# A hybrid decoder block: the first tap and the edge columns of its short convolution move from VectorE to ScalarE

## The chip, the core and the metric

The kernel runs on one core of a Trainium2 chip. The metric is the device time of one execution in microseconds (us), given as the median of several runs. A core has one matrix engine (TensorE; PE in the profile, its weight loads PEld), three engines for element work (VectorE or DVE, ScalarE or ACT, GpSimd or POOL) and a queue that issues the transfers (SyncE or SP). Each engine works through its own instructions in the order in which they stand in its queue and waits, where needed, for semaphores of the others.

## What is computed

One decoder layer on 2048 positions of width 1024, in float32. Both head groups, the output projection, a SwiGLU feed-forward part and three RMS norms are in it. The part that matters here is head group B, a gated causal convolution of width 3 over positions:

```python
h = rmsnorm(x, norm1_g[l])
proj = h @ w_in[l]
p_q, p_k, p_v, p_g, p_a, c_b, c_c, c_h = jnp.split(proj, splits, axis=-1)
...
o = gla_chunked(q, k, v, log_a)          # head group A
...
u = c_c * c_h
o_conv = c_b * causal_depthwise_conv(u, conv_w[l])
mixed = jnp.concatenate([o_gla, o_conv], axis=-1) @ w_out[l]
x = x + mixed
...
def causal_depthwise_conv(u, w):
    """u: (B,S,C), w: (CONV_K, C). y_t = sum_j w_j * u_{t-(CONV_K-1)+j}."""
    u_pad = jnp.pad(u, ((0, 0), (CONV_K - 1, 0), (0, 0)))
    y = w[0] * u_pad[:, 0:seq]
    for j in range(1, CONV_K):
        y = y + w[j] * u_pad[:, j:j + seq]
```

So position t needs u at t-2, t-1 and t: a block of positions needs the last two columns of the block to its left.

## The kernel before

Channels lie on the 128 partitions and positions on the free axis. The 2048 positions are four blocks of 512 (`PB`), handled as two halves of two blocks. In `in_proj(half, ops, first)` twelve *units* run one after the other. A unit multiplies 256 output channels with both blocks of the half by a scheme of seven 512-wide block products instead of eight (`PRODUCTS`, `unit`, lines 344 to 382). Each product is a run of 12 matmuls of 128x512: float32 is split into a high and a low part (`split`, line 144), and for each k the order is high·high (line 340), high·low (line 341), low·high (line 342). The weights of a unit are split when they have arrived: ScalarE copies the high part (line 145), VectorE subtracts it for the low part (line 146), and GpSimd builds the sums that the scheme needs (lines 323, 324, 325 and 330). Products that are read out go from PSUM to SBUF on ScalarE (line 360) or are added on VectorE (line 364). A PSUM bank can be written again only after it has been read, so TensorE waits for these.

The last six units are the convolution: for `i0` = 0 and 2 the units of c_c, c_h and c_b. After the unit of c_h a loop runs over two channel tiles (`r`) and the two blocks of the half (`j`). It multiplies u = c_c * c_h into a tile of 514 columns (line 577), copies the two columns on the left from `halo` (line 578), copies the tile's own last two columns back into `halo` (line 579), forms the first tap into y (line 581), which takes the place of c_c, and adds the second and third tap (line 583). That makes four passes of four tiles; in time they lie at 210 to 238, 271 to 296, 491 to 521 and 573 to 594 us. After the unit of c_b the result is multiplied with it (line 588), split and stored (lines 590 to 593) for the output projection.

Beside the units run pieces of background work that `tick()` advances after each product: `h1_ahead` (norm and split of the second half's input, with `scaled` on line 464, GpSimd differences on lines 246 to 259 and `split`), the forget gate (`forget_gate`, lines 531 to 550) and the chunks of the linear attention (`gla_half`: scores on line 640, transposes on lines 646, 649 and 700, outputs on lines 664 and 666, state on lines 681 and 682, carry on line 656, norm on lines 688 to 693). The program is not issued in source order: a scheduler with its own timeline orders each engine's queue when the program is built, so an edit at one place can move instructions of the units and of the background work around it. The feed-forward part (`ffn_up`, `ffn_down`) follows from about 855 us on.

Waits of TensorE that the prediction names belong to these names: `wq` is a split weight quarter (`weight_quarter`), `c` a product that was read out, `raw` the weights as they come from memory, `osb` a normalised chunk of the attention that is transposed on line 700.

Of the kernel before, what the change touches and what calls it, by code (L numbers as in the profile page):

```python
# [13 lines left out]
AF = mybir.ActivationFunctionType  # L14
ALU = mybir.AluOpType
# [6 lines left out]
PB = 512  # L22
# [20 lines left out]
C_G1, C_G2, C_GF, C_BG, C_GN, C_CW = 0, 8, 16, 24, 26, 27  # L43
# [4 lines left out]
def tile_hymba_block(ctx, tc, x, xt, win, wa, wgu, wout, wffn, wdown, wdown_first, small, out):  # L48
    nc = tc.nc
    act, dve, pool, pe = nc.scalar, nc.vector, nc.gpsimd, nc.tensor  # L50
# [42 lines left out]
    halo = mixer.tile([P, 4, 2], F32, name="halo")  # L93
# [30 lines left out]
    def col(c):  # L124
        return sml[:, c : c + 1]
# [13 lines left out]
    def store(dst, src):  # L139
        return nc.sync.dma_start(dst, src)  # L140
# [3 lines left out]
    def split(src, hi, lo):  # L144
        last_hi[:] = [act.activation(hi, src, AF.Copy)]  # L145
        return dve.tensor_tensor(lo, src, hi.bitcast(F32), ALU.subtract)  # L146
# [197 lines left out]
    def unit(src, ops, into=None):  # L344


        w = unit_weights(src)

        def mul(i, o=None):
            first = o is None  # L350
            o = bank() if first else o
            n, m = PRODUCTS[i]
            for k in range(len(ops[m])):
                product_step(o, w[n], ops[m], k, first)
            tick()
            return o

        def copied(name, o, at):
            t = tt(name) if into is None else into[at]
            act.activation(t[:], o[:], AF.Copy)  # L360
            return t

        def plus(t, o):
            dve.tensor_tensor(t[:], o[:], t[:], ALU.add)  # L364
            return t


        oa = mul(0)
        c11 = copied("c11", oa, (0, 0))
        ob = mul(1)  # L370
        c22 = copied("c22", ob, (1, 1))
        mul(2, oa)
        c12 = copied("c12", oa, (0, 1))
        plus(c11, mul(3))
        mul(4, oa)
        plus(c22, oa)
        mul(5, ob)
        plus(c12, ob)
        mul(6, oa)
        if into is not None:  # L380
            copied("c21", oa, (1, 0))
        return [(0, 0, c11, False), (1, 1, c22, False), (0, 1, c12, False), (1, 0, oa, True)]

    def settled(c, in_psum):

        if not in_psum:
            return c
        s = tt("c11")
        act.activation(s[:], c[:], AF.Copy)
        return s  # L390
# [3 lines left out]
    def silu(c, in_psum):  # L394
        s = tt("sg") if in_psum else c
        last_silu[:] = [act.activation(s[:], c[:], AF.Silu)]
        return s
# [156 lines left out]
    def in_proj(half, ops, first):  # L554
        def units():
            for u in range(12):
                with ExitStack() as stack:
                    if half == 0 and u == 1:
                        stack.enter_context(tc.issue_after(last_load[0].ins))
                    yield first if u == 0 and first else unit(win[u], ops)  # L560

        units = units()
        for dst, i0 in ((s_kq, 0), (s_kq, 2), (s_v, 0), (s_v, 2)):
            for r, j, c, p in next(units):
                store(dst[2 * half + j][i0 + r][:], settled(c, p)[:])
        for i0 in (0, 2):
            for r, j, c, p in next(units):
                store(s_g[2 * half + j][i0 + r][:], silu(c, p)[:])
        background.append(gla_half(half))
        for i0 in (0, 2):  # L570
            cc = {(r, j): settled(c, p) for r, j, c, p in next(units)}
            ch = {(r, j): c for r, j, c, _ in next(units)}
            for r in range(2):
                i = i0 + r
                for j in range(2):
                    s = tp.tile([P, PB + 2], F32, name="u", tag="t")
                    dve.tensor_tensor(s[:, 2:], ch[r, j][:], cc[r, j][:], ALU.mult)
                    dve.tensor_copy(s[:, 0:2], halo[:, i, :])
                    dve.tensor_copy(halo[:, i, :], s[:, PB : PB + 2])
                    y = cc[r, j]  # L580
                    dve.tensor_scalar(y[:], s[:, 0:PB], col(C_CW + i), None, ALU.mult)
                    for n in (1, 2):
                        dve.scalar_tensor_tensor(
                            y[:], s[:, n : n + PB], col(C_CW + 4 * n + i), y[:], ALU.mult, ALU.add
                        )
            for r, j, c, _ in next(units):
                y = cc[r, j]
                dve.tensor_tensor(y[:], c[:], y[:], ALU.mult)
                hi = tp.tile([P, PB], F32R, name="hi", tag="t")
                split(y[:], hi[:], y[:].bitcast(F32R))  # L590
                dst = s_mix[2 * half + j][i0 + r]
                store(dst[:, 0, :], hi[:].bitcast(F32))
                store(dst[:, 1, :], y[:])


    def gla_half(half):
        chunks = [(b, t) for b in (2 * half, 2 * half + 1) for t in range(PT)]
        with tc.issue_after(last_silu[0].ins):
            tables = act.preload_act_table_set("natural_log_exp_and_others")
        with tc.issue_after(tables.ins):  # L600
            nxt = gla_load(*chunks[0])
        o = None
        for n, (b, t) in enumerate(chunks):
            cur = nxt
            s = gla_scores(b, t, *cur)
            yield
            if o is not None:
                gla_finish(*chunks[n - 1], *o)
                yield
            if n + 1 < len(chunks):  # L610
                nxt = gla_load(*chunks[n + 1])
            o = gla_outputs(b, t, *s)
            yield
        gla_finish(b, t, *o)
        done.add((b, t))
        yield
# [315 lines left out]
    def last_unit(src, ops, b12, y, ssq):  # L932
# [62 lines left out]
        ]  # L995
    )
    in_proj(0, ops, first)
    drain_background(lambda: len(background) < 2)
    ops = load_pairs(s_h1)
    background.append(gate(1, ops))  # L1000
    in_proj(1, ops, None)
    drain_background(lambda: (1, PT - 1) in done)
    ssq = out_proj(0, build_mix(0))
# [118 lines left out]
```

## Time and profile before

| | us |
|---|---|
| median of 3 runs | 2133.78 (2132.6 to 2134.49) |
| the profiled execution | 2132.17 |
| span of the profiled execution | 2130.3 |
| mean granted TensorE clock in it | 0.986 of full speed |
| matmuls of the units, lines 340 to 342, busy | 984.6 + 977.6 + 969.8 |
| ScalarE product copies, line 360, busy | 156.3 (270 of them) |
| VectorE additions of products, line 364, busy | 185.0 (270 of them) |

The profile holds one execution. Rows of a timeline read: start, duration, engine, line, operation, output<-input, shapes and types, and in brackets the idle time of the engine just before it with what ended it. Rows of a table by stretches of time read: the stretch, its length, then the busy time of PE, PEld, DVE, ACT and POOL with the number of instructions, the granted clock, the share of the transfer engines and GB/s; a table restricted to one line shows only the engines that the line uses. A row of a line reads: duration in ns as minimum/median/maximum, and when the first and the last started.

### The profile page before, as it was taken

How to read it: one execution, taken by the hardware profiler on the slowest of the kernel's cores; microseconds unless marked ns; L12 is line 12 of the kernel's file. 1: busy time of each engine (PE TensorE's matmuls, PEld its weight loads, DVE VectorE, ACT ScalarE, POOL GpSimd, SP SyncE). 2: the span in 40 equal slices, each digit the busy share in tenths (PEclk: the TensorE clock that was granted, in tenths of full speed). 3: DMA queues.
4: the chain of work that ended last, by engine and by line, in shares of the span. 5: the costliest groups of instructions: out<-in, count | busy, mean ns of one | idle time of the engine just before them, and what ended most of it. 6: DMA issues, size and time to landing. Idle time of an engine off the chain costs nothing.

```text
span 2130.3 us, 26959 instructions
## 1 busy us (share of the span) xinstructions
PE 2048.0 (96%) x9137; PEld 1656.0 (78%) x9137; DVE 1435.2 (67%) x2035; ACT 1005.8 (47%) x1959; POOL 983.5 (46%) x707
## 2 busy tenths in 40 slices
PE   6899999999999999999999999999999999999996
PEld 4677787887788887778788887887888888887875
DVE  7768875558663586887887564554786777664554
ACT  6455344565543334654555453333454454553344
POOL 3526422221102364555555346874644555435774
PEclk9999999999999999999999999999999999999998
DMA  7349587433495981655554577698365445587662
GB/s 281 114 136 328 189 314 228 149 105 110 145 334 175 362 297 70 212 230 195 222 218 180 219 301 265 246 348 351 125 221 204 151 176 197 190 333 276 267 266 109
DMA packets 190987, 470.80 MB, mean 221 GB/s; under 512 B 19968, under 2 KB 65280, under 8 KB 181248
## 3 DMA queue, kind: packets, MB, share of 16 engines
q1 hardware_dynamic: 190848, 469.07, 60.9%
q8 instruction: 72, 1.18, 0.2%
q14 instruction: 67, 0.55, 0.1%
HBM read 300.70 MB, written 168.30 MB: 220 GB/s over the span
## 4 chain that ended last, share of the span: by engine, by line
PE 76%; DMA 9%; DVE 8%; ACT 3%; issue 2%; POOL 1%; SPq 1%; DVEq 0%; ACTq 0%; POOLq 0%
PE mm L340 22%; PE mm L342 22%; PE mm L341 22%; DVE wq L146 2%; PE mm L740 2%; PE mm L741 2%; PE mm L743 2%; DVE op L146 1%; DVE h L464 1%; DMA op<-sa_B 1%; DMA raw<-in_wdown_dram 1%; DMA op<-shT 1%; PE a_ps L515 1%; DVE so L146 1%; DMA sx<-y 1%
## 5 line engine op out<-in xcount | busy, mean ns | idle before, releaser
L340 PE MATMUL mm<-op,wq 128*128 128x512 f32 x2495 | 984.6, 396 | 27.7 <-ACT c L360 16.9
L342 PE MATMUL mm<-op,wq 128*128 128x512 f32 x2495 | 969.8, 394 | 16.1 <-DVE wq L146 15.4
L341 PE MATMUL mm<-op,wq 128*128 128x512 f32 x2495 | 977.6, 392 | 1.1 <-DVE op L146 1.1
L146 DVE TENSOR_TENSOR wq<-raw,wq 128x512 fp32r<-128x512 f32 (+2 forms) x628 | 533.6, 855 | 306.8 <-ACT wq L145 304.3
L145 ACT ACTIVATE wq<-raw 128x512 fp32r<-128x512 f32 (+2 forms) x628 | 366.7, 588 | 583.2 <-PE mm L342 422.8
L340 PEld LDWEIGHTS mm<-op,wq 128*128 128x128 f32 x2495 | 472.1, 189 | 147.9 <-ACT c L360 22.8
L342 PEld LDWEIGHTS mm<-op,wq 128*128 128x128 f32 x2495 | 472.1, 189 | 126.1 <-DVE wq L146 26.8
L341 PEld LDWEIGHTS mm<-op,wq 128*128 128x128 f32 x2495 | 472.7, 189 | 99.0 <-DVE op L146 1.9
L325 POOL TENSOR_TENSOR raw<-s,raw 128x512 f32<-128x512 f32 (+2 forms) x98 | 128.5, 1312 | 439.4 <-DVE wq L146 392.4
L364 DVE TENSOR_TENSOR c<-mm,c 128x512 f32<-128x512 f32 x270 | 185.0, 685 | 114.0 <-PE mm L342 111.4
L323 POOL TENSOR_TENSOR s<-raw 128x512 f32<-128x512 f32 (+2 forms) x98 | 131.1, 1338 | 190.6 <-DMA raw<-in_wffn_dram 91.4
L330 POOL TENSOR_TENSOR raw<-raw 128x512 f32<-128x512 f32 (+2 forms) x98 | 128.1, 1307 | 139.0 <-DVE wq L146 118.2
L360 ACT ACTIVATE c<-mm 128x512 f32<-128x512 f32 x270 | 156.3, 585 | 29.9 <-PE mm L342 29.2
L722 POOL TENSOR_TENSOR ssx<-ssx,q 128x512 f32<-128x512 f32 x52 | 75.1, 1457 | 152.5 <-ACT q L721 152.4
L324 POOL TENSOR_TENSOR raw<-raw 128x512 f32<-128x512 f32 (+2 forms) x98 | 138.3, 1411 | 4.5
L902 POOL TENSOR_TENSOR y<-c,y 128x512 f32<-128x512 f32 x66 | 99.2, 1505 | 68.5 <-DVE c L364 68.4
L146 DVE TENSOR_TENSOR so<-t,so 128x512 fp32r<-128x512 f32 x100 | 95.1, 959 | 20.5 <-ACT so L145 20.4
L145 ACT ACTIVATE wq<-s 128x512 fp32r<-128x512 f32 (+2 forms) x98 | 57.6, 587 | 97.1 <-PE mm L342 94.6
L740 PE MATMUL mm<-op,wq 128*128 128x512 f32 x256 | 100.7, 394 | 0.0
L741 PE MATMUL mm<-op,wq 128*128 128x512 f32 x256 | 99.8, 390 | 0.0
L146 DVE TENSOR_TENSOR wq<-s,wq 128x512 fp32r<-128x512 f32 (+2 forms) x98 | 83.8, 855 | 15.5 <-ACT wq L145 15.1
L145 ACT ACTIVATE so<-t 128x512 fp32r<-128x512 f32 x100 | 62.6, 628 | 44.8 <-DMA sa_B<-so 21.6
(173 smaller groups left out, 1884.3 us busy)
## 6 DMA issues: line engine op xcount, KB each, us to landing
raw<-in_wffn_dram SPq DMA_DIRECT2D x44, 1024.0 KB, 5.9
sa_T<-so SPq DMA_DIRECT2D x88, 512.0 KB, 4.6
op<-sa_T SPq DMA_DIRECT2D x88, 512.0 KB, 9.6
sa_B<-so SPq DMA_DIRECT2D x69, 512.0 KB, 3.4
op<-sa_B SPq DMA_DIRECT2D x69, 512.0 KB, 9.3
raw<-in_win_dram SPq DMA_DIRECT2D x23, 1024.0 KB, 5.4
raw<-in_wdown_dram SPq DMA_DIRECT2D x24, 768.0 KB, 5.8
sx<-y SPq DMA_DIRECT2D x48, 256.0 KB, 4.6
```

The lines of the kernel that those rows point to most:

```text
L145: last_hi[:] = [act.activation(hi, src, AF.Copy)]
L146: return dve.tensor_tensor(lo, src, hi.bitcast(F32), ALU.subtract)
L323: pool.tensor_tensor(s1, a21, a22, ALU.add)
L324: pool.tensor_tensor(a21, a11, a21, ALU.subtract)
L325: pool.tensor_tensor(a11, s1, a11, ALU.subtract)
L340: pe.matmul(o[:], wh, xh, start=first and k == 0, stop=False, skip_group_check=True)
L341: pe.matmul(o[:], wh, xl, start=False, stop=False, skip_group_check=True)
L342: return pe.matmul(o[:], wl, xh, start=False, stop=k == n - 1, skip_group_check=True)
L360: act.activation(t[:], o[:], AF.Copy)
L364: dve.tensor_tensor(t[:], o[:], t[:], ALU.add)
L740: pe.matmul(o[e, j][:], wh, m[:, 0, :], start=k == 0, stop=False)
L741: pe.matmul(o[e, j][:], wh, m[:, 1, :], start=False, stop=False)
```

## The change

The first tap becomes a ScalarE copy with a per-partition scale, and the copies of the two edge columns become ScalarE copies. The second block of a half (`j` = 1) takes its two left columns from the first block's tile `s` rather than from `halo`, and `halo` is written once for each channel tile, after both blocks, and in the first half only. The product, the second and third tap and everything else are as they were; lines below the edit shift by three.

```diff
@@ -572,17 +572,20 @@
             for r in range(2):
                 i = i0 + r
+                left = halo[:, i, :]
                 for j in range(2):
                     s = tp.tile([P, PB + 2], F32, name="u", tag="t")
                     dve.tensor_tensor(s[:, 2:], ch[r, j][:], cc[r, j][:], ALU.mult)
-                    dve.tensor_copy(s[:, 0:2], halo[:, i, :])
-                    dve.tensor_copy(halo[:, i, :], s[:, PB : PB + 2])
+                    act.activation(s[:, 0:2], left, AF.Copy)
+                    left = s[:, PB : PB + 2]
                     y = cc[r, j]
-                    dve.tensor_scalar(y[:], s[:, 0:PB], col(C_CW + i), None, ALU.mult)
+                    act.activation(y[:], s[:, 0:PB], AF.Copy, scale=col(C_CW + i))
                     for n in (1, 2):
                         dve.scalar_tensor_tensor(
                             y[:], s[:, n : n + PB], col(C_CW + 4 * n + i), y[:], ALU.mult, ALU.add
                         )
+                if half == 0:
+                    act.activation(halo[:, i, :], left, AF.Copy)
```

## The prediction

> **What bounds the kernel now.** I read the page's busy shares first, then its chain of waits, then a table of stretches around the four convolution passes, and last the timeline of each engine inside them.
>
> ```profile
> PE 2048.0 (96%) x9137; PEld 1656.0 (78%) x9137; DVE 1435.2 (67%) x2035; ACT 1005.8 (47%) x1959; POOL 983.5 (46%) x707
> PE 76%; DMA 9%; DVE 8%; ACT 3%; issue 2%; POOL 1%; SPq 1%; DVEq 0%; ACTq 0%; POOLq 0%
> 200.00:240.00 40.00, 35.69 (x141) 27.70 (x141) 38.99 (x59) 17.44 (x32) 19.35 (x12) 0.91 0.77 257
> 270.00:295.00 25.00, 25.00 (x119) 20.47 (x118) 20.95 (x40) 8.42 (x16) 5.90 (x4) 1.00 0.72 266
> 485.00:520.00 35.00, 34.16 (x143) 26.11 (x142) 29.53 (x59) 15.79 (x32) 5.76 (x4) 1.00 0.26 81
> 520.00:545.00 25.00, 22.63 (x130) 18.45 (x129) 21.43 (x40) 14.40 (x37) 5.72 (x4) 1.00 0.60 195
> 570.00:595.00 25.00, 25.00 (x134) 20.54 (x133) 23.48 (x55) 12.81 (x37) 3.75 (x2) 1.00 0.72 247
> ```
>
> TensorE is busy for 96% of the span and carries the chain, so VectorE time is worth something only where TensorE waits for it. The first number after a stretch is its length, the second TensorE's busy time. In the second and fourth pass (270 to 295, 570 to 595) TensorE is busy throughout: nothing can be gained there. The first pass (200 to 240, VectorE 39 of 40 us) leaves 4.3 us of gaps, and its granted clock is 0.91. The third leaves 0.8 us; behind it, at 520 to 545, lie 2.4 us. The timeline names these gaps; the bracket is the wait before the row and what ended it:
>
> ```profile
> 217.47 0.50 PE L342 MATMUL mm<-op,wq 128*128 128x512 f32 x1 [0.62 <-DVE wq L146]
> 226.03 0.50 PE L342 MATMUL mm<-op,wq 128*128 128x512 f32 x1 [2.82 <-DVE wq L146]
> 227.63 0.63 PE L342 MATMUL mm<-op,wq 128*128 128x512 f32 x1
> 230.18 0.80 PE L340 MATMUL mm<-op,wq 128*128 128x512 f32 x1 [0.64 <-ACT c L360]
> 233.76 0.62 PE L342 MATMUL mm<-op,wq 128*128 128x512 f32 x1
> 515.75 0.50 PE L342 MATMUL mm<-op,wq 128*128 128x512 f32 x1 [0.84 <-DVE wq L146]
> 539.62 0.50 PE L340 MATMUL mm<-op,wq 128*128 128x512 f32 x1 [2.37 <-ACT c L360]
> 873.76 0.50 PE L342 MATMUL mm<-op,wq 128*128 128x512 f32 x1 [3.01 <-DVE wq L146]
> 874.10 0.40 PE L340 MATMUL mm<-op,wq 128*128 128x512 f32 x1
> ```
>
> So 0.62 + 2.82 + 0.64 + 0.84 + 2.37 = 7.3 us of waits are within reach. One thing hangs on them. After the wait of 2.82 the matmuls from 227.63 to 233.76 last 0.63 instead of 0.40: the lower clock costs (1 - 0.91) x 35.69 = 3.2 us. After the wait of 3.01 at 873.76 the next one lasts 0.40, and the stretch that holds the wait of 2.37 has a clock of 1.00. A wait of this length therefore sometimes brings the slow clock and sometimes not; I treat it as a chance event of one execution.
>
> The Trainium skill, "TensorE: Matmul & The Clock Gate", section "HAM oscillation — how this bites in real kernels", puts the limit at gaps above about 3.4 us; its section "What's actually happening" says that the activity window is free-running. By the first, 2.82 would have cost no clock and shortening it would be worth its length alone; the trace disagrees there, and the rows decide. The second would explain why 3.01 went unpunished.
>
> **What the change removes and adds.** The rows of the removed lines, then the nearest rows for what ScalarE gets:
>
> ```profile
> L578 DVE COPY u<-halo x16: 151/158/1294, 211.1 to 587.9; 128x2 f32<-128x2 f32 x16
> L579 DVE COPY halo<-u x16: 151/158/1268, 212.4 to 589.8; 128x2 f32<-128x2 f32 x16
> L581 DVE TENSOR_SCALAR c<-u,sml x16: 470/476/1593, 213.2 to 589.8; 128x512 f32<-128x512 f32 x16
> L942 ACT ACTIVATE y<-y,sml 128x512 f32<-128x512 f32 x16 | 11.2, 715 | 0.2
> L150 ACT ACTIVATE hl<-hsq 128x4 f32<-128x4 f32 x16 | 3.3, 206 | 3.5 <-DVE hsq L689 3.2
> ```
>
> By medians VectorE loses 16 x (0.158 + 0.158 + 0.476) = 12.7 us. ScalarE gains 16 taps, 16 left copies and 4 halo writes (two channel tiles for each of the first half's two passes): 16 x 0.715 + 20 x 0.206 = 15.6 us, 3.9 us a pass. Line 942 is the same operation, size and per-partition scale as the tap; the bounds of a tap are 0.58 (product copies of this width, 156.3 us over 270) and 0.72. ScalarE is free for 22.6 of 40, 16.6 of 25, 19.2 of 35 and 12.2 of 25 us in the passes' rows, so 3.9 us fit into each; that idle time is the cover. If it were gone, all 15.6 us would lie on ScalarE's queue ahead of weight halves and product copies. No transfer is added or removed, and PE and transfers differ in order only near the passes; the feed-forward part issues as before.
>
> **First pass.** What ends the wait of 2.82 is the last low part of a weight quarter, VectorE's 225.29 row:
>
> ```profile
> 218.68 0.68 DVE L364 TENSOR_TENSOR c<-mm,c 128x512 f32<-128x512 f32 x1
> 219.28 1.64 DVE L146 TENSOR_TENSOR lo<-t,hi 128x512 fp32r<-128x512 f32 x1
> 220.84 1.78 DVE L146 TENSOR_TENSOR wq<-raw,wq 128x512 fp32r<-128x512 f32 x1
> 222.54 1.24 DVE L579 COPY halo<-u 128x2 f32<-128x2 f32 x1
> 223.69 0.47 DVE L581 TENSOR_SCALAR c<-u,sml 128x512 f32<-128x512 f32 x1
> 224.09 1.28 DVE L146 TENSOR_TENSOR lo<-h,hi 128x512 fp32r<-128x512 f32 x2
> 225.29 0.68 DVE L146 TENSOR_TENSOR wq<-raw,wq 128x512 fp32r<-128x512 f32 x1
> 219.08 1.29 POOL L323 TENSOR_TENSOR s<-raw 128x512 f32<-128x512 f32 x1 [3.09 <-DMA raw<-in_win_dram]
> 220.44 1.62 POOL L324 TENSOR_TENSOR raw<-raw 128x512 f32<-128x512 f32 x1
> 222.03 1.72 POOL L259 TENSOR_TENSOR t<-h,t 128x512 f32<-128x512 f32 x1
> ```
>
> Three VectorE operations here take about 1.1 us too long (1.64 and 1.78 against 0.68; the two-column copy 1.24 against 0.158), each while a GpSimd operation runs: the engines take turns. What VectorE can give back is therefore its own operations, not the turns of GpSimd, which stay three. In the changed program the queue behind the 218.68 addition holds five operations up to the awaited one: a low part, a quarter, a low part, a second tap, the quarter. Before it held seven: a low part, a quarter, copy, first tap, two low parts, the quarter. One low part moved ahead (0.62 by starts), copy (0.08 by its pitch) and tap (0.40) left, one second tap (0.68) came in: 0.62 + 0.08 + 0.40 - 0.68 = 0.4 us earlier. The tap waits on ScalarE for the product u; behind it in that queue stand the high parts of the next quarters, due about 2.5 us later by my walk, so they stay covered. Bounds: the whole wait goes (-2.8), or a GpSimd turn more, half a piece long, slips in (+0.5). I take -0.4, nearest the summed rows. The 0.62 before it gains at most itself, but it lies ahead of the same second wait, which then grows by as much: 0. The 0.64 for a product copy stays.
>
> **Third pass.** The awaited quarter is VectorE's 515.02 row:
>
> ```profile
> 510.91 1.27 DVE L579 COPY halo<-u 128x2 f32<-128x2 f32 x1
> 515.02 0.68 DVE L146 TENSOR_TENSOR wq<-raw,wq 128x512 fp32r<-128x512 f32 x1
> ```
>
> A copy of 1.27 leaves the queue ahead of it, but its turn with GpSimd passes to its neighbour; with one tap's 0.40 and 0.08 for the copy it is 0.5 us earlier: -0.5 (bounds -0.84, all of it; +0.3, a ScalarE tap late by 0.715 against VectorE's 0.47).
>
> **Behind the third pass.** The wait of 2.37 ends with a product copy that stands in ScalarE's queue behind the attention's carry, and that waits for VectorE's state:
>
> ```profile
> 529.05 2.98 DVE L146 TENSOR_TENSOR c<-c,hi 128x512 fp32r<-128x512 f32 x3
> 531.95 1.78 DVE L146 TENSOR_TENSOR wq<-raw,wq 128x512 fp32r<-128x512 f32 x1
> 534.18 1.47 DVE L146 TENSOR_TENSOR c<-c,hi 128x512 fp32r<-128x512 f32 x1
> 536.60 0.81 ACT L656 ACTIVATE carry<-state,em 64x128 f32<-64x128 f32 x2 [3.29 <-DVE state L682]
> 536.87 0.39 PE L342 MATMUL mm<-op,wq 128*128 128x512 f32 x1
> 538.99 0.58 ACT L360 ACTIVATE c<-mm 128x512 f32<-128x512 f32 x1
> 539.73 0.68 DVE L693 TENSOR_TENSOR osb<-o_ps,hsq 128x512 f32<-128x512 f32 x1
> ```
>
> Here the scheduler's new order matters more than the tap. VectorE's state (before it: a quarter of 1.78 and a low part of 1.47) moves ahead of both, so carry can start some 3 us earlier; but TensorE's next work at 537.26 is now the four transposes of `osb` (line 700) instead of a product, and `osb` was ready only at 539.73 + 0.68 = 540.41. Walking the new VectorE and ScalarE queues with these rows, `osb` is done at about 538.2 to 538.5: a wait of 1.0 to 1.3 in place of 2.37. The product behind needs a copy that by then is done. I take -1.2; bounds -2.37 (`osb` ready in time) and +0.8 (540.41 - 537.26 = 3.15 against 2.37, `osb` no earlier than now).
>
> **The sum.** -0.4 - 0.5 - 1.2 = -2.1 us. The profiled execution took 2132.17, so 2130.1. The shown runs have a median of 2133.78, 1.6 higher, a spread that the clock's chance alone could make; I keep to the profiled execution's time.
>
> **The rivals.**
> 1. *The slow clock no longer follows the first pass's wait*, because a wait of 2.4 brings it less often. For it: 873.76 and 539.62. Against it: 0.4 us is little. 2132.17 - 2.1 - 3.2 = 2126.9.
> 2. *The first pass's waits go altogether*: if the turns with GpSimd fall elsewhere when its two subtractions move ahead. 2132.17 - (0.62 + 2.82 + 0.64) - 3.2 - 0.5 - 1.2 = 2123.2. Against it: VectorE is full there (39 of 40), and 3.2 us a pass is little of it.
> 3. *The freed time does not reach TensorE at all*: the two engines' turns sum to the same, and at 537 one wait replaces the other. 2132.2.
> 4. *Slower: the transposes moved forward.* `osb` as late as now makes 3.15 of 2.37 (+0.8), and a wait that long brings the slow clock of 3.2: 2132.17 + 0.8 + 3.2 = 2136.2 without the other gains. It is slower than before from the point where `osb` is done later than 539.63. Against it: the state is 3 us earlier in the queue.
> 5. *Slower: the tap as a link that shows.* Each is 0.715 - 0.476 = 0.24 longer; all 16 on the path would give 2132.17 + 3.8 = 2136.0. Against it: in the second and fourth pass TensorE waits for nothing, and ScalarE is idle for half of each. [...]
>
> **How the numbers follow.** Chances: forecast 0.32, rivals in order 0.20, 0.12, 0.16, 0.10 and 0.05; 0.05 for a wait that no row shows, slower too. The forecast's own range is 2128 to 2132.5. The bounds of the terms reach from 2132.17 - 2.8 - 0.84 - 2.37 - 3.2 = 2123.0 to 2132.17 + 0.5 + 0.3 + 0.8 + 3.2 = 2137.0, and that is the range; outside it lie half of rival 2 and most of the unseen waits. About 0.2% (4.3 us) is what a measurement of this kernel tells from no change, so faster means under 2129.5: rivals 1 and 2 and a third of the forecast, 0.43. Slower means above 2138.05: the unseen waits and a third of rivals 4 and 5, 0.10. Within: 0.47.
>
> **What would show it.** TensorE's wait in the first pass should be 2.3 to 2.6 with VectorE's quarter as releaser; the clock row of 200 to 240 tells forecast from rival 1. The wait near 515 should be 0.2 to 0.5. Near 537 the releaser should be `osb`, with 1.0 to 1.3. VectorE's total should fall by 12 to 21 us, ScalarE's rise by 15 to 16. A TensorE wait released by a tap, or in the second or fourth pass, or any difference behind 855 us that is more than a shift, would prove it wrong.

## The result and the profile after

The changed kernel takes 2127.95 us (median of 9 runs, 2122.54 to 2131.03) against 2134.24 us (9 runs, 2131.71 to 2136.05): ratio 0.9974, 95% interval 0.9963 to 0.9984; the medians differ by 6.3 us, the ratio is 5.5 us with an interval of 3.4 to 7.9. In a later set of runs (12 against 35 of the kernel before) the same program gave 0.9972 (0.9961 to 0.9983), 6.0 us. The profiled execution took 2128.85 us.

Page of the changed kernel: busy times and the chain of waits.

```profile
PE 2043.6 (96%) x9137; PEld 1651.9 (78%) x9137; DVE 1426.8 (67%) x1987; ACT 1018.1 (48%) x1995; POOL 977.8 (46%) x707
PE 75%; DVE 9%; DMA 9%; ACT 3%; issue 2%; SPq 1%; POOL 1%; DVEq 0%; ACTq 0%; POOLq 0%
```

VectorE gave up 8.4 us and ScalarE took on 12.3. Stretches of the changed kernel, cut as before the change:

```profile
200.00:240.00 40.00, 36.73 (x157) 28.82 (x157) 37.70 (x48) 21.36 (x43) 18.56 (x12) 1.00 0.75 255
485.00:520.00 35.00, 34.82 (x144) 26.53 (x144) 28.45 (x50) 19.32 (x42) 5.54 (x4) 1.00 0.25 82
520.00:545.00 25.00, 24.17 (x138) 19.59 (x138) 21.19 (x39) 14.37 (x37) 5.81 (x4) 1.00 0.67 220
```

The clock in the first pass is 1.00 instead of 0.91, and TensorE's gaps behind the third pass fell from 2.4 to 0.8 us. The first pass lies some 4 us later in this execution, so its row does not hold quite the same work as the row of before. TensorE's main waits in its timeline, changed kernel:

```profile
228.91 0.50 PE L342 MATMUL mm<-op,wq 128*128 128x512 f32 x1 [2.30 <-DVE wq L146]
231.81 0.50 PE L340 MATMUL mm<-op,wq 128*128 128x512 f32 x1 [0.31 <-ACT c L360]
252.17 0.50 PE L340 MATMUL mm<-op,wq 128*128 128x512 f32 x1 [0.58 <-ACT c L360]
516.03 0.50 PE L342 MATMUL mm<-op,wq 128*128 128x512 f32 x1 [0.18 <-DVE wq L146]
538.63 0.66 PE L703 MATMUL ot<-ident,osb 128*128 128x128 f32 x4 [0.83 <-DVE osb L696]
```

Each answers to a row of before: 2.82 became 2.30 with the same releaser, 0.84 became 0.18, and the product copy's 2.37 became 0.83 for the normalised chunk `osb`, whose transposes now come first. New is 0.58 near 252.

Whole executions differ by several microseconds, so the two places are better compared by a *stretch* of their own: from one product copy on line 360 to another, with the same products between them. First the kernel before, then the changed one (timeline of ScalarE):

```profile
204.58 0.59 ACT L360 ACTIVATE c<-mm 128x512 f32<-128x512 f32 x1
254.20 0.60 ACT L360 ACTIVATE c<-mm 128x512 f32<-128x512 f32 x1 [2.03 <-PE mm L342]
455.13 0.58 ACT L360 ACTIVATE c<-mm 128x512 f32<-128x512 f32 x1
561.42 0.58 ACT L360 ACTIVATE c<-mm 128x512 f32<-128x512 f32 x1
```

```profile
208.36 0.59 ACT L360 ACTIVATE c<-mm 128x512 f32<-128x512 f32 x1
255.21 0.60 ACT L360 ACTIVATE c<-mm 128x512 f32<-128x512 f32 x1 [2.08 <-PE mm L342]
456.08 0.58 ACT L360 ACTIVATE c<-mm 128x512 f32<-128x512 f32 x1
560.32 0.58 ACT L360 ACTIVATE c<-mm 128x512 f32<-128x512 f32 x1
```

Stretch 1 (round the first pass) is 254.20 - 204.58 = 49.62 us before and 46.85 after; stretch 2 (third pass and what lies behind it) is 106.29 before and 104.24 after. Between the two stretches nothing differs: 200.9 us in every one of the profiles. The same differences, from the same rows of every profile, with VectorE's busy time and the granted clock in stretch 1 beside them:

| kernel | ratio to before (95%) | stretch 1 | VectorE busy in it | clock in it | stretch 2 |
|---|---|---|---|---|---|
| before, first profile | | 49.62 | 47.70 | 0.93 | 106.29 |
| before, second | 0.9995 (0.9981 to 1.0008) | 49.32 | 47.41 | 0.93 | 105.35 |
| before, third | | 48.74 | 46.94 | 1.00 | 105.34 |
| changed, first profile | 0.9974 as above | 46.85 | 44.42 | 1.00 | 104.24 |
| changed, second | 0.9972 as above | 46.91 | 44.45 | 1.00 | 104.08 |
| changed, third | | 47.10 | 44.66 | 1.00 | 104.25 |
| taps alone | 0.9985 (0.9975 to 0.9995) | 48.59 | 44.38 | 0.96 | 103.30 |
| copies alone | 0.9988 (0.9976 to 1.0000) | 50.40 | 47.04 | 0.97 | 104.25 |
| first half only | 0.9997 (0.9986 to 1.0008) | 47.03 | 44.59 | 1.00 | 107.84 |
| second half only | 0.9990 (0.9981 to 1.0000) | 49.04 | 47.27 | 0.97 | 103.98 |
| copies on VectorE | 0.9975 (0.9962 to 0.9987) | 48.20 | 45.22 | 0.93 | 104.03 |
| differences on VectorE | 0.9980 (0.9968 to 0.9992) | 47.04 | 45.26 | 1.00 | 103.97 |
| mixed | 0.9972 (0.9959 to 0.9984) | 46.85 | 44.41 | 1.00 | 104.19 |
| load put back | 0.9986 (0.9975 to 0.9997) | 49.84 | 48.06 | 1.00 | 104.22 |

In the eight profiles with a clock of 1.00, stretch 1 is VectorE's busy time plus 1.8 to 2.5 us. By the means of three profiles the change gains 49.23 - 46.95 = 2.3 us in stretch 1 and 105.66 - 104.19 = 1.5 us in stretch 2: 3.8 us. Against the one profile of before with the full clock, stretch 1 gains 48.74 - 46.95 = 1.8 us. The three profiled spans are 2130.3, 2126.6, 2125.5 against 2127.1, 2120.0, 2124.6, means 2127.5 and 2123.9, 3.6 us.

### The profile page after: what moved, and what is told of

It is laid out like the page before. It is cut to its first block, busy times and chain, and to the rows that moved or that the text cites. A ratio compares the mean times of both kernels' runs of the same rounds, so it can differ in the third digit from the quotient of the medians.

```text
span 2127.1 us, 26939 instructions
## 1 busy us (share of the span) xinstructions
PE 2043.6 (96%) x9137; PEld 1651.9 (78%) x9137; DVE 1426.8 (67%) x1987; ACT 1018.1 (48%) x1995; POOL 977.8 (46%) x707
## 4 chain that ended last, share of the span: by engine, by line
PE 75%; DVE 9%; DMA 9%; ACT 3%; issue 2%; SPq 1%; POOL 1%; DVEq 0%; ACTq 0%; POOLq 0%
PE mm L340 22%; PE mm L342 22%; PE mm L341 21%; DMA raw<-in_wdown_dram 2%; PE mm L743 2%; PE mm L744 2%; PE mm L746 2%; DVE wq L146 2%; DVE h L464 2%; DVE op L146 1%; DMA op<-sa_B 1%; DVE so L146 1%; DMA op<-shT 1%; PE a_ps L515 1%; SPq L137 1%
## 5 line engine op out<-in xcount | busy, mean ns | idle before, releaser
L323 POOL TENSOR_TENSOR s<-raw 128x512 f32<-128x512 f32 (+2 forms) x98 | 129.5, 1321 | 205.4 <-DMA raw<-in_wffn_dram 99.2
```

The lines of the kernel that those rows point to most:

```text
L323: pool.tensor_tensor(s1, a21, a22, ALU.add)
```

## The experiments

**Taps alone.** First taps on ScalarE, copies and `halo` as before.

```diff
-                    dve.tensor_scalar(y[:], s[:, 0:PB], col(C_CW + i), None, ALU.mult)
+                    act.activation(y[:], s[:, 0:PB], AF.Copy, scale=col(C_CW + i))
```

> Only the first taps go to ScalarE; the copies and the halo stay on VectorE. If VectorE's time in the first pass is what counts (theory), the taps carry most of it: the two-column copies cost 0.08 us of pitch each, but may draw a GpSimd turn of 1.1 us. Expected: the quarter's wait near 226 at 2.3 to 2.8, 2.5 to 5 us faster than before. If the copies' dependency through halo is what counts (rival), this run gains less than 1 us and the run with the copies alone has the gain.

Measured: 0.9985, 3.2 us faster. Its waits:

```profile
222.03 0.50 PE L340 MATMUL mm<-op,wq 128*128 128x512 f32 x1 [0.48 <-DVE c L364]
227.55 0.50 PE L342 MATMUL mm<-op,wq 128*128 128x512 f32 x1 [2.03 <-DVE wq L146]
232.31 0.50 PE L340 MATMUL mm<-op,wq 128*128 128x512 f32 x1 [0.87 <-ACT c L360]
```

The time is within the expected 2.5 to 5 us, but not for the expected reason. The quarter's wait is 2.03, under the expected 2.3, yet stretch 1 gained only 0.6 us on the mean of before. VectorE was as little busy in it as in the changed kernel (44.38 us), but stood idle for 4.2 us instead of 2.4. Two of its rows show where, both behind ScalarE, the first behind the tap itself:

```profile
233.39 0.75 DVE L583 SCALAR_TENSOR_TENSOR c<-u,sml,c 128x512 f32<-128x512 f32 x1 [0.81 <-ACT c L581]
251.16 0.70 DVE L146 TENSOR_TENSOR wq<-raw,wq 128x512 fp32r<-128x512 f32 x1 [1.26 <-ACT wq L145]
```

Stretch 2 gained 2.4 us, more than with the whole change, mostly because TensorE's transposes of `osb` stand there without a wait:

```profile
537.80 0.60 PE L700 MATMUL ot<-ident,osb 128*128 128x128 f32 x4
```

**Copies alone.** The changed kernel's copies and columns, with the taps on VectorE.

```diff
-                    act.activation(y[:], s[:, 0:PB], AF.Copy, scale=col(C_CW + i))
+                    dve.tensor_scalar(y[:], s[:, 0:PB], col(C_CW + i), None, ALU.mult)
```

> Only the copies go to ScalarE and the second block takes its columns from the first block's tile; the first taps stay on VectorE. Theory: 0 to 2 us faster than before, with the wait near 226 at 2.4 to 2.8. Rival (the chain through halo held VectorE): 4 us or more.

Measured: 0.9988, 2.6 us faster, between theory and rival; the interval reaches 1.0000.

```profile
223.18 0.50 PE L340 MATMUL mm<-op,wq 128*128 128x512 f32 x1 [0.98 <-DVE c L364]
227.57 0.50 PE L342 MATMUL mm<-op,wq 128*128 128x512 f32 x1 [0.90 <-DVE wq L146]
252.65 0.50 PE L340 MATMUL mm<-op,wq 128*128 128x512 f32 x1 [1.91 <-ACT c L360]
519.17 0.50 PE L342 MATMUL mm<-op,wq 128*128 128x512 f32 x1 [1.24 <-DVE wq L146]
```

The quarter's wait fell to 0.90, well under the 2.4 to 2.8 expected, and stretch 1 was longer than in the kernel before, not shorter. VectorE is busy 47.04 us in it, no less than in the kernel before at full clock (46.94). Behind the wait of 1.91 seven matmuls of 0.63 start 0.43 us apart instead of 0.23, when VectorE has little left to do: about 1.4 us, by this estimate most of what the stretch is longer. Stretch 2 is as short as with the whole change in spite of the wait of 1.24; here too the transposes of `osb` (540.78) stand without a wait. So either part alone brings the new order behind the third pass. In both partial kernels a single wait said nothing of the length of its pass.

**First half only, second half only.** The changed loop stands under a condition (`half == 1` in the second kernel), the old one under its `else`.

```diff
+            if half == 0:
...
+            else:
...
```

> The whole change, but in the first half of the positions only (passes at 210 and 271 us). Theory: the first pass gains 0.9 us of waits and the slow clock's 3.4 us in the executions where it would have come; 1 to 4.5 us faster. The waits near 516 (0.84) and near 540 (2.37, ended by a product copy) stay. Rival (the gain comes from the second half's new order): 0 us.

> The whole change, but in the second half only (passes at 491 and 573 us). Theory: the wait near 516 falls from 0.84 to 0.2, the one near 540 from 2.37 to 0.8 with the normalised attention chunk as releaser, together 2.2 us; the waits of 0.62, 2.82 and 0.64 in the first pass stay. 2 to 3 us faster, more where a wait of 2.37 would have brought the slow clock. Rival (all of it is the first pass): 0 us.

Timelines of TensorE behind the third pass, first half only, then second half only:

```profile
516.26 0.50 PE L342 MATMUL mm<-op,wq 128*128 128x512 f32 x1 [0.83 <-DVE wq L146]
540.14 0.50 PE L340 MATMUL mm<-op,wq 128*128 128x512 f32 x1 [2.38 <-ACT c L360]
```

```profile
514.84 0.50 PE L342 MATMUL mm<-op,wq 128*128 128x512 f32 x1 [0.18 <-DVE wq L146]
537.16 0.66 PE L718 MATMUL ot<-ident,osb 128*128 128x128 f32 x4 [0.57 <-DVE osb L711]
```

The waits follow the half that is changed, as expected: 0.83 and 2.38 stay in the one, 0.18 and 0.57 on `osb` come in the other. So do the stretches: 47.03 in stretch 1 with the first half changed, 103.98 in stretch 2 with the second, while 49.04 in stretch 1 of the latter stays at the value of before. The 107.84 of the first has a slow clock in it, behind its wait of 2.38:

```profile
540.82 0.63 PE L342 MATMUL mm<-op,wq 128*128 128x512 f32 x1
543.38 0.63 PE L342 MATMUL mm<-op,wq 128*128 128x512 f32 x1
```

The first profile of the kernel before had the same wait without it and took 106.29, so here it cost about 1.55 us. The times are less clear. The second half alone is 2.1 us faster; the first half alone is 0.6 us faster with an interval of 3.0 us faster to 1.7 slower, where 1 to 4.5 was expected. Together that is less than the whole change's 5.5 to 6.0, though within the intervals.

**The same programs again.**

> The changed kernel once more, on the same chip as the runs of this call. If its first gain of 0.26% is the waits (theory: 2.2 us behind the second half's passes, under 1 us in the first pass, the rest the chance of the slow clock), it is 2 to 5 us faster than before here, and in its profile the waits near 516 and 538 (0.2 and 0.8, the latter on the normalised chunk) come back to the hundredth, while the slow windows lie elsewhere. Rival (the first pass gives most of it): 5 us or more again.

> The kernel before, against itself: what two sets of runs of one program differ by, and which waits of its first profile come back. Theory: 0.84 near 516 and 2.37 near 540 return; those of the first pass (0.62, 2.82, 0.64) vary by some tenths with the arrival of the weights; slow windows of 3.4 us follow some of the waits of 2.0 to 3.1 us and not others.

Against itself the kernel before gave 0.9995 with 1 inside the interval. The changed kernel gave 0.9972, 6.0 us of 2132, with an interval of 3.6 to 8.3: the gain is there again. The value lies above the theory's 2 to 5 us, where its rival put it; the interval reaches into both. Waits of the second profiles, before and changed:

```profile
225.71 0.50 PE L342 MATMUL mm<-op,wq 128*128 128x512 f32 x1 [2.74 <-DVE wq L146]
515.36 0.50 PE L342 MATMUL mm<-op,wq 128*128 128x512 f32 x1 [0.84 <-DVE wq L146]
538.31 0.50 PE L340 MATMUL mm<-op,wq 128*128 128x512 f32 x1 [1.42 <-ACT c L360]
```

```profile
225.95 0.50 PE L342 MATMUL mm<-op,wq 128*128 128x512 f32 x1 [2.27 <-DVE wq L146]
513.11 0.50 PE L342 MATMUL mm<-op,wq 128*128 128x512 f32 x1 [0.18 <-DVE wq L146]
535.55 0.66 PE L703 MATMUL ot<-ident,osb 128*128 128x128 f32 x4 [0.71 <-DVE osb L696]
```

The 0.18 came back, the 0.83 as 0.71. The 2.37 did not return: it was 1.42 here and 1.41 in the third profile, and 2.38 in the kernel with the first half changed. The first profile had shown the larger of two values.

**Copies on VectorE.** The changed kernel, columns still from the first block's tile, copies on VectorE.

```diff
-                    act.activation(s[:, 0:2], left, AF.Copy)
+                    dve.tensor_copy(s[:, 0:2], left)
...
-                    act.activation(halo[:, i, :], left, AF.Copy)
+                    dve.tensor_copy(halo[:, i, :], left)
```

> The change with its copies on VectorE (columns still from the first block's tile, halo still written once): 24 copies less VectorE relief than the changed kernel has. If the copies' engine is without weight (theory, 0.08 us of pitch each), the same as the changed kernel within 2 us. Rival: the copies' turns with GpSimd (1.24 us in the first pass) come back and with them 2 us or more.

Measured: 0.9975, the changed kernel's gain. In the time, no weight of the engine that copies the two columns shows, with an interval of about 2.7 us to each side. The one profile is less even: stretch 1 is 48.20, 1.25 us above the changed kernel's mean, with VectorE 0.7 us busier and a slow clock behind a longer wait for the quarter:

```profile
229.27 0.79 PE L342 MATMUL mm<-op,wq 128*128 128x512 f32 x1 [3.14 <-DVE wq L146]
```

So a small weight of the copies in the first pass is not excluded. Where the columns come from and the fewer writes of `halo` are part of this kernel, so they aren't judged by it.

**Differences on VectorE.** The changed kernel with lines 246 to 259 on VectorE for the second half's input.

```diff
-            pool.tensor_tensor(t1[:], b12[:], b11[:], ALU.subtract)
+            sub.tensor_tensor(t1[:], b12[:], b11[:], ALU.subtract)
...
-        yield from combine(lambda k, j: xt[2 + j, :, k, :], C_G1, (rbs[2], rbs[3]), put)
+        yield from combine(lambda k, j: xt[2 + j, :, k, :], C_G1, (rbs[2], rbs[3]), put, dve)
```

> The changed kernel with the 16 GpSimd differences of the second half's input (in the first half's units) on VectorE. If turns with GpSimd hold up VectorE in the first pass (theory), each moved difference costs VectorE 0.62 and saves a turn of about 1.1: the quarter's wait of 2.30 falls to about 1.0 to 1.8, 0.5 to 3 us faster than the changed kernel. Rival (VectorE's own load is the bound): three to four more operations ahead of the quarter, the wait grows to about 4 us.

Measured: 0.9980, no better than the changed kernel, and stretch 1 is 47.04. The timeline of TensorE:

```profile
229.24 0.50 PE L340 MATMUL mm<-op,wq 128*128 128x512 f32 x1 [2.04 <-ACT c L360]
250.48 0.50 PE L340 MATMUL mm<-op,wq 128*128 128x512 f32 x1 [1.89 <-ACT c L360]
```

The quarter's wait has gone, further than the theory of turns had it, but not the time: 2.04 and 1.89 on product copies stand in its place. In stretch 1 GpSimd has 8 operations instead of 12, and VectorE, with the four moved ones, is busy 45.26 us instead of 44.4 to 44.7: a difference costs VectorE little more than its turn did.

**Mixed, and third profiles.** The whole change in the first half, the taps alone in the second (`else`), and one more profile of each of the two programs.

```diff
+            if half == 0:
...
+            else:
...
+                        dve.tensor_copy(s[:, 0:2], halo[:, i, :])
+                        dve.tensor_copy(halo[:, i, :], s[:, PB : PB + 2])
+                        y = cc[r, j]
+                        act.activation(y[:], s[:, 0:PB], AF.Copy, scale=col(C_CW + i))
```

> The whole change in the first half, only the taps in the second (its copies on VectorE, through halo). The changed kernel gained about 2.5 us in the first pass, and the run with the taps alone gained about 3 us between 485 and 560 us against 2.1 of the changed kernel, because its queue left no wait near 540. If the two parts add up (theory), this is 5 to 6 us faster than before and up to 0.9 us faster than the changed kernel; no wait above 0.4 between 500 and 560. Rival (the scheduler orders the second half anew once the first half differs): the wait of 0.6 to 0.9 on the normalised chunk is there and the gain is that of the changed kernel or less.

> The kernel before, one more look. If the first pass's long wait of 2.7 to 2.8 brings the slow clock nearly always (theory), there are slow windows right behind 226 again; if it is an even chance (rival), this one may well be without. The wait of 0.84 near 515 returns.

> The changed kernel, one more look. Theory: a wait of 2.3 in the first pass without a slow window behind it, and 0.7 to 0.85 on the normalised chunk near 537. Rival (an even chance): a slow window behind the wait of 2.3.

The mixed kernel is as fast as the changed one (0.9972) and has its wait on `osb` (0.61), so its rival holds: the order that left no wait near 540 didn't come with it. The third profile of the kernel before had no slow clock in the first pass, so it does not follow nearly always. Stretch 1 in the first profile, then in the third:

```profile
204.58:254.20 49.62, 45.31 (x183) 35.70 (x182) 47.70 (x72) 20.66 (x40) 20.04 (x12) 0.93 0.71 233
```

```profile
203.56:252.30 48.74, 42.35 (x182) 33.77 (x182) 46.94 (x71) 20.39 (x40) 20.55 (x12) 1.00 0.70 234
```

TensorE is busy 3.0 us less at the full clock for the same matmuls (183 and 182 records), but the stretch is only 0.9 us shorter: the rest went into waits. The timeline of the third profile names them:

```profile
216.21 0.50 PE L342 MATMUL mm<-op,wq 128*128 128x512 f32 x1 [0.38 <-DVE wq L146]
224.30 0.50 PE L342 MATMUL mm<-op,wq 128*128 128x512 f32 x1 [2.37 <-DVE wq L146]
228.46 0.50 PE L340 MATMUL mm<-op,wq 128*128 128x512 f32 x1 [1.59 <-ACT c L360]
249.22 0.50 PE L340 MATMUL mm<-op,wq 128*128 128x512 f32 x1 [1.43 <-ACT c L360]
```

Where the slow clock was, the wait for the product copy behind it was 0.64 and there was none near 249. In the changed kernel's third profile the waits were 1.01, 1.41, 0.33 and 0.56 in place of 2.30, 0.31 and 0.58, with a stretch 1 of 47.10 against 46.85: the waits are shuffled, the length stays. It had no slow clock there either; the wait on `osb` was 0.84, as expected.

**Load put back.** The changed kernel, the first tap written twice more by VectorE, in the first pass only.

```diff
                     act.activation(y[:], s[:, 0:PB], AF.Copy, scale=col(C_CW + i))
+                    for _ in range(2 if half == 0 and i0 == 0 else 0):
+                        dve.tensor_scalar(y[:], s[:, 0:PB], col(C_CW + i), None, ALU.mult)
```

> The changed kernel, with the first tap repeated twice on VectorE (same value written) for the four tiles of the first pass only: eight operations of 0.40 us of pitch, 3.2 us, more than the 2.2 us that the change took from that pass (four taps at 0.40, eight copies at 0.08). Theory (the first pass runs at VectorE's pace, so its length follows VectorE's work there, wherever the single waits show): from 200 to 260 us the gain of about 2 us is gone and the pass is 0.5 to 1.5 us longer than in the kernel before; in all 2.5 to 4 us slower than the changed kernel, with about 2 us left against the kernel before from the second half, whose wait on the normalised chunk stays at 0.6 to 0.9. Rival (only the operations ahead of the awaited quarters count): less than 1 us slower than the changed kernel.

Measured: 0.9986 against 0.9972 of the changed kernel: 3.0 us of 6.0 are gone, though the two intervals overlap. Firmer is the stretch. The rows on ScalarE, then on TensorE:

```profile
205.84 0.59 ACT L360 ACTIVATE c<-mm 128x512 f32<-128x512 f32 x1
255.68 0.60 ACT L360 ACTIVATE c<-mm 128x512 f32<-128x512 f32 x1 [2.10 <-PE mm L342]
```

```profile
252.62 0.50 PE L340 MATMUL mm<-op,wq 128*128 128x512 f32 x1 [2.53 <-ACT c L360]
539.14 0.66 PE L705 MATMUL ot<-ident,osb 128*128 128x128 f32 x4 [0.87 <-DVE osb L698]
```

Stretch 1 is 49.84, 2.9 us above the changed kernel's mean, for 3.2 us of VectorE work, and 1.1 us above the kernel before at full clock, where 0.5 to 1.5 was expected; stretch 2 is unchanged. VectorE is busy 48.06 us, 1.1 more than in that profile of the kernel before: the length moved by as much. The long wait stands near 252, on a product copy, and not at a quarter.

## Why the prediction came out as it did

The direction held and the measured 2127.95 lies in the range 2123 to 2137, but the forecast of 2.1 us (2130.1) was too small: the runs show 5.5 (3.4 to 7.9). That is above 0.2%, which had 0.43 of the chances.

**The failing step is the first pass's -0.4.** It counted only the operations ahead of one awaited quarter (0.62 + 0.08 + 0.40 - 0.68). That wait came out as forecast in two profiles of three (2.30, 2.27 and 1.41, forecast 2.3 to 2.6), yet stretch 1 became 2.3 us shorter. VectorE's relief in the whole pass is four taps at 0.40 and eight copies at 0.08, 2.2 us. Full clock against full clock, 1.8 us of it arrived; the other 0.5 us of the 2.3 is the slow clock in two of before's three profiles. I had the row (VectorE 38.99 of 40.00) and used it against rival 2, where it says that the pass is as long as VectorE's work. The run with load put back shows this: 3.2 us in, 2.9 us longer. It holds only as long as VectorE isn't made to wait: the taps alone gave 0.6 us for their 1.6, because VectorE stood idle behind ScalarE, partly behind a tap, and the copies alone left VectorE as busy as before. Why the queues came out so in these two wasn't followed up.

**The 0.62 at 217 costed at 0** has gone as a wait of its own; like the others there it can't be priced by itself.

**Rival 1's 3.2 us for the slow clock** was mis-sized. By the prediction's own sign, the clock row of 200 to 240, this rival came in (1.00 instead of 0.91), and its 2126.9 is the nearest of all to the measured 2127.95. That nearness is luck: the kernel before has the slow clock in two profiles of three, and without it stretch 1 is 0.6 to 0.9 us shorter, not 3.2: the product copies' waits of 1.59 and 1.43 take its place. Its absence in the changed kernel's first pass is not the main part of the gain. Rival 2 fell: the quarter's wait did not go.

**Third pass and behind it**: -0.5 and -1.2 forecast. The waits fell from 0.84 to 0.18 and from 2.37 to 0.83 on `osb`, with the forecast's releaser, a little below the 1.0 to 1.3 that the walk gave: 0.7 and 1.5 against the profiled execution. Against all three profiles stretch 2 gained 1.5 us. That this is near the forecast 1.7 is partly luck: `osb` came earlier than walked, and the 2.37 was the larger of its two values. That the new order matters more than the tap is borne out: the taps alone and the copies alone both bring it. Rival 4 fell: `osb` came earlier, and the wait at its transposes is under 0.9 in every profile. Rivals 3 and 5 fell with the sign; no wait in the changed kernel's list is ended by a tap, and the second and fourth pass have none.

**Engine totals.** VectorE fell by 8.4 us, not 12 to 21. The removed rows had held 20.7 us, but other operations took up the turns with GpSimd that these had waited for. Busy time of the second and third taps, kernel before and changed kernel:

```profile
0.00:2131.00 2131.00, 24.87 (x32) 0.99 0.61 221
```

```profile
0.00:2131.00 2131.00, 29.71 (x32) 0.99 0.61 221
```

That is 4.8 us more with nearly the same median (0.741 and 0.745 us): only the long ones beside GpSimd became more. ScalarE's own rows came out as priced (a tap 0.719 against 0.715, a small copy 0.190 against 0.206, together 15.3 us), and the durations of all its rows add up to 15.3 us more, yet its total rose by 12.3. Neighbouring operations overlap in its timeline (a copy of 0.58 at 212.91 is followed by a start at 213.39), and the total seems to count such time once.

**What stays open.** The two stretches give 3.8 us, the timed runs 5.5 and 6.0, with intervals that begin at 3.4 and 3.6. That the profiled spans give 3.6 is no confirmation, since two parts outside the stretches cancel in them. The changed kernel comes to stretch 1 at 208.4, 205.4 and 206.3 us instead of 204.6, 204.6 and 203.6, 2.4 us later on the mean, and from the end of stretch 2 to the last instruction it takes 1566.8, 1562.8 and 1566.0 us instead of 1568.9, 1566.5 and 1567.0, 2.3 us less. Whether this is chance or a difference behind 855 us, which the prediction had named as a sign against itself, three profiles don't tell. No version tried was clearly faster than the changed kernel.

## What to carry to other kernels

Where an engine is busy for 39 of 40 us of a stage, price a change there by all the work that it takes from this engine in the stage, and don't stop at the operations ahead of one wait: its releasers and places change from profile to profile, while the stage's length stays. Check too that the engine isn't made to wait for the one that took the work over. Measure a stage between two operations that both kernels have, such as two product copies, and profile each kernel more than once before a wait of one profile goes into a sum.

## What the runs showed of the hardware

A slow clock can be nearly free. In the first pass twelve matmuls of 0.63 us cost 0.6 to 0.9 us net, since the operands that they would have waited for were late anyway; behind 540 seven of them cost about 1.55. The Trainium skill, "TensorE: Matmul & The Clock Gate", section "HAM oscillation — how this bites in real kernels", warns of idle gaps above about 3.4 us; here waits of 2.82, 2.74 and 2.69 near 226 were followed by a lower clock, as were 2.03 and 1.91 in the partial kernels, while 3.01 at 871 in the changed kernel was not:

```profile
871.25 0.50 PE L342 MATMUL mm<-op,wq 128*128 128x512 f32 x1 [3.01 <-DVE wq L146]
871.59 0.40 PE L340 MATMUL mm<-op,wq 128*128 128x512 f32 x1
```

The measurement decides: gaps below 3.4 us can bring it. Whether one does varies from execution to execution, of one program too: this wait of 3.0 us stands near 870 in all 14 profiles, and the clock between 862 and 882 us is 0.91 in seven of them and 1.00 in the other seven (kernel before: 1.00, 0.91, 1.00). On small copies: the two columns cost 0.19 to 0.20 us on ScalarE, and on VectorE 0.15 to 1.29 us, according to whether GpSimd was at work.
